# Squares in wide operations, a conditioning visit and the transposes at other places, and the samples' modulation on VectorE, in a decoder step on one core

## The chip, the cores and the metric

The kernel runs on one NeuronCore of a Trainium2 chip. The metric is the device time in microseconds (us) of one execution. In the profile PE is TensorE (PEld its weight loads), DVE is VectorE, ACT is ScalarE, POOL is GpSimd, and SP is the engine that issues most DMAs. All five run their own instruction list strictly in its order and wait for each other through semaphores.

## The reference

One layer for 256 prompt tokens and 8 x 4 sample tokens (288 columns in all), width 2048. Each of the nine sequences (one prompt, eight samples) has its own conditioning row `c`. Cut to what the change touches:

```python
mod = (silu(c) @ w_ada + b_ada)            # per sequence: 6 x 2048
sh_m, sc_m, gt_m, sh_f, sc_f, gt_f = split(mod)
h = rms(x, g_mix) * (1 + sc_m) + sh_m
proj = h @ w_in                            # 2048 x 9216: b, c, hc, u, v, ga, gb
ya = b * short_conv(c * hc)
u, v = gelu(u), rms(gelu(v), g_v)          # v by rows of tokens: its transpose is needed
yb = u * (causal(w_sg) @ v + b_sg)
merged = sigmoid(ga) * (ya @ w_pa) + sigmoid(gb) * (yb @ w_pb)
x = x + gt_m * (merged @ w_out)
h2 = rms(x, g_ffn) * (1 + sc_f) + sh_f
x = x + gt_f * ((silu(gate(h2)) * up(h2)) @ w_ffn_out)
y = rms(x, g_final)
```

## The kernel before

Activations lie transposed, 16 tiles `x[:, k, :]` of 128 features by 288 tokens. Every large product is done in three passes of rounded fp32 parts: `triple` issues three matmuls of 288 columns (lines 214, 215 and 216). The weight's parts come from `Blk.split`: ACT casts 512 columns of a `raw` tile into `hi` (line 393), DVE subtracts to get `lo` (line 395). There are four `hi` and four `lo` buffers, four PSUM banks for products (`pm`), three for small results (`px`), one for the conditioning product (`ada`), and a ring of seven `raw` tiles of 1 MB into which the weights are loaded ahead.

The steps run as a list. TensorE's order is written by hand; the order on the other engines is chosen when the program is built, and is fixed after that. The list begins so:

- `warm` issues matmuls on a constant (line 454) while the first loads are under way.
- `squares1` squares the 16 tiles of x, on DVE (line 461) and ACT (line 463) in turns, and sums each over the features with three one-column matmuls into one PSUM bank (line 465). `roots` makes the reciprocal root from it (DVE line 191, POOL line 194), and `norm1` spreads that over the partitions (line 203) and copies it to `rb` (line 478).
- `Ada` steps multiply conditioning rows by blocks of `w_ada` (line 329). Their `tail` copies the result (`ev`, line 344), turns it on TensorE (line 351), and adds the bias into `mod` (line 355). A run of such steps between two products is called a visit below. `aA` gives shift and scale of tile 0 only, `aB` those of tiles 1 and 2, `aC` those of tiles 3 to 6, `aD` of 7, and `aE` of 8 to 15.
- `mk_h1` makes `gm` (line 486) and calls `modulate`: per tile a product with `rb` (line 247, DVE), the affine step of the 256 prompt columns (lines 257 and 258, ACT), that of the 32 sample columns (lines 261 and 262, POOL), a cast (line 266, ACT) and a subtraction (line 271, DVE). `mk_h2` calls the same for the second half of the layer, 16 tiles, while the four `KBlk` steps of `fk` run.
- The product with `w_in` is cut by input tiles so that it can start before the conditioning is done: six blocks `wA` use tile 0 alone (eight output tiles each, one triple per output tile), then `wB` uses tiles 1 and 2, `wX` 0 to 2, `wC` 3 to 7, `wD` 8 to 15. The first ones write `part` (lines 503 and 505, ACT and DVE), later ones add to it (line 508). `at` says after how many blocks a visit stands.
- In the `wD` stage `sinkD` calls `mix_conv` for 8 output tiles (a dozen DVE operations each, lines 533 to 548). `mix_conv` copies the samples' conv state from the constants `cp` into `zs` (line 537), a copy that needs nothing else. `v_transpose` queues 12 pairs of transposes (line 569), one pair after every second triple, and a DVE operation empties each pair's `px` bank (line 571).

Loads: `load_x`, then the first seven steps' `raw` tiles, with the second pack of constants `cp` behind `wA[0]` (line 797). Each later step's tile is loaded seven steps ahead, as soon as its place in the ring is free.

## Time and profile before

| | |
|---|---|
| runs | 1675.88, 1673.26, 1675.97 us; median 1675.88 |
| profiled execution | 1675.97 us, of which the span of its instructions is 1674.2 us |
| PE busy | 1650.9 us |
| DVE busy | 988.3 us |
| ACT busy | 743.4 us |
| POOL busy | 45.7 us |

A row of the timeline gives the start in us, the duration, the engine, the source line, the operation, output and inputs, and in brackets how long the engine had been idle and what ended that. A PE matmul's shown end is modelled, so busy PE time also holds stretches at a low rate; starts are what to read there. A row of the windows gives for each engine the busy time and the number of instructions in a stretch, and the clock that TensorE was granted. Line numbers of the profile are those of the kernel before.

### The profile page before, as it was taken

The numbers are of one execution on the slowest core, as the hardware profiler recorded it, in microseconds if no ns is written. First come the engines' busy times: TensorE is split into PE (matmuls) and PEld (weight loads), VectorE is DVE, ScalarE is ACT, GpSimd is POOL, SyncE is SP. The second block draws the span as 40 slices with busy tenths as digits, with TensorE's granted clock in tenths as the row PEclk, the third lists the DMA queues.
The fourth block names the chain that finished last, engine by engine and source line by source line (L and its number), as shares of the span: only waits on it lengthen the run. The fifth ranks groups of instructions, "written<-read, shape, count | busy, mean of one in ns | idle before, by whom it ended". The sixth has DMA issues, their size and how long they took to land.

```text
span 1674.2 us, 31388 instructions
## 1 busy us (share of the span) xinstructions
PE 1650.9 (99%) x12584; PEld 1582.2 (95%) x12584; DVE 988.3 (59%) x2011; ACT 743.4 (44%) x1373; POOL 45.7 (3%) x126
## 2 busy tenths in 40 slices
PE   9999999999999999999999999999999999999997
PEld 8899999998989999899989999999999999999997
DVE  3675556877755566667854455555555555555565
ACT  3444334543344434446734444444444444444453
POOL 0000001000000000002300000000000000000000
PEclk9999999999999999999999999999999999999998
DMA  6776776766678666664478546453464534654341
GB/s 267 280 294 236 303 279 244 267 249 234 255 285 325 253 225 251 253 242 163 152 283 308 205 157 218 163 173 116 156 217 169 168 121 156 214 173 159 116 155 57
DMA packets 57266, 357.61 MB, mean 214 GB/s; under 512 B 6400, under 2 KB 9376, under 8 KB 24352
## 3 DMA queue, kind: packets, MB, share of 16 engines
q1 hardware_dynamic: 56832, 355.38, 58.3%
q8 instruction: 98, 1.61, 0.4%
q14 instruction: 48, 0.39, 0.1%
q10 hardware_dynamic: 288, 0.22, 0.0%
HBM read 352.49 MB, written 3.09 MB: 212 GB/s over the span
## 4 chain that ended last, share of the span: by engine, by line
issue 50%; PE 47%; DVE 1%; ACT 1%; POOL 1%; DMA 0%; POOLq 0%; DVEq 0%; ACTq 0%
PE pm L214 14%; PE pm L216 13%; PE pm L215 13%; PE ada L329 4%; PE px L465 1%; DVE x L722 0%; DVE lo L395 0%; PE px L351 0%; PE px L203 0%; POOL t L261 0%; DMA ct<-in_c 0%; ACT hi L393 0%; POOL t L262 0%; PE px L609 0%; PE px L611 0%
## 5 line engine op out<-in xcount | busy, mean ns | idle before, releaser
L214 PE MATMUL pm<-s,hi 128*128 128x288 f32 (+1 forms) x3760 | 1115.1, 297 | 5.3 <-ACT s L503 2.6
L216 PE MATMUL pm<-s,lo 128*128 128x288 f32 (+1 forms) x3760 | 1111.2, 296 | 0.2 <-DVE lo L395 0.2
L215 PE MATMUL pm<-s,hi 128*128 128x288 f32 (+1 forms) x3760 | 1109.5, 295 | 0.0
L393 ACT CAST hi<-raw 128x512 fp32r<-128x512 f32 (+1 forms) x966 | 588.6, 610 | 814.1 <-PE pm L215 778.9
L395 DVE TENSOR_TENSOR lo<-raw,hi 128x512 fp32r<-128x512 f32 (+1 forms) x966 | 655.4, 679 | 492.4 <-ACT hi L393 477.6
L214 PEld LDWEIGHTS pm<-s,hi 128*128 128x128 f32 x3760 | 708.0, 188 | 23.7 <-issue 15.3
L215 PEld LDWEIGHTS pm<-s,hi 128*128 128x128 f32 x3760 | 708.4, 188 | 0.2 <-DVE s L271 0.2
L216 PEld LDWEIGHTS pm<-s,lo 128*128 128x128 f32 x3760 | 707.9, 188 | 0.4 <-DVE lo L395 0.4
L329 PE MATMUL ada<-raw,cs 128*32 128x512 f32 (+2 forms) x960 | 89.6, 519 | 0.0
L508 DVE TENSOR_TENSOR s<-pm,s 128x288 f32<-128x288 f32 x120 | 54.2, 454 | 41.2 <-PE pm L216 41.1
L329 PEld LDWEIGHTS ada<-raw,cs 128*32 128x32 f32 x960 | 29.1, 113 | 43.7 <-issue 38.5
L516 DVE TENSOR_TENSOR s<-pm,s 128x288 f32<-128x288 f32 x72 | 32.8, 456 | 15.9 <-PE pm L216 15.8
L240 ACT CAST s<-t 128x288 fp32r<-128x288 f32 (+1 forms) x76 | 32.6, 432 | 16.1 <-DVE t L548 7.4
L242 DVE TENSOR_TENSOR s<-t,s 128x288 fp32r<-128x288 f32 (+1 forms) x76 | 34.5, 458 | 6.4 <-ACT s L240 6.4
L287 DVE SCALAR_TENSOR_TENSOR x<-pm,mod,x 128x256 f32<-128x256 f32 x80 | 38.0, 475 | 0.0
L694 DVE SCALAR_TENSOR_TENSOR t<-t,pm 128x288 f32<-128x288 f32 x42 | 19.1, 454 | 16.2 <-PE pm L216 16.2
L286 DVE TENSOR_TENSOR t<-pm,mod 128x32 f32<-128x32 f32 x80 | 15.3, 192 | 22.0 <-PE pm L216 22.0
L194 POOL TENSOR_TENSOR r<-e,mhalf 128x3 f32<-128x3 f32 x4 | 3.4, 858 | 899.0 <-DVE e L193 873.5
L153 ACT ACTIVATE t<-x 128x288 f32<-128x288 f32 x30 | 13.4, 445 | 20.8 <-DVE x L288 20.8
L465 PEld LDWEIGHTS px<-ones,t 128*128 128x128 f32 x96 | 20.6, 333 | 1.5 <-ACT t L463 1.5
L465 PE MATMUL px<-ones,t 128*128 128x1 f32 x96 | 20.6, 352 | 1.0 <-ACT t L463 1.0
L158 DVE TENSOR_TENSOR acc<-acc,t 128x288 f32<-128x288 f32 x34 | 15.5, 455 | 8.2 <-ACT t L153 8.2
(108 smaller groups left out, 455.3 us busy)
## 6 DMA issues: line engine op xcount, KB each, us to landing
raw<-in_fi SPq DMA_DIRECT2D x84, 1024.0 KB, 4.9
raw<-in_a SPq DMA_DIRECT2D x64, 1024.0 KB, 9.9
raw<-in_f SPq DMA_DIRECT2D x64, 704.0 KB, 4.0
raw<-in_wD SPq DMA_DIRECT2D x36, 1024.0 KB, 5.0
raw<-in_wC SPq DMA_DIRECT2D x24, 960.0 KB, 4.9
raw<-in_aE SPq DMA_DIRECT2D x16, 1024.0 KB, 8.7
raw<-in_wo SPq DMA_DIRECT2D x16, 1024.0 KB, 5.0
raw<-in_aC SPq DMA_DIRECT2D x8, 1024.0 KB, 8.8
```

Source lines behind the costliest of these rows:

```text
L214: PE.matmul(out, wh, ah, start=first, stop=False)
L215: PE.matmul(out, wh, al, start=False, stop=False)
L216: lh = PE.matmul(out, wl, ah, start=False, stop=last)
L240: A.copy(hi, a)
L242: V.tensor_tensor(lo, a, hi.bitcast(F32), ALU.subtract)
L287: V.scalar_tensor_tensor(x[:, m, :TP], ps[:, :TP], mod[:, gt0 + m, 0:1], x[:, m, :TP], ALU.mult, ALU.add)
L329: PE.matmul(acc[32 * j : 32 * j + 32, :w], cs[:, kt, :], self.raw[:, o : o + w], start=(kt < ks), stop=(kt >= 16 - ks), tile_position=(0, ...
L393: A.copy(hi, self.raw[:, s * 128 : e * 128])
L395: V.tensor_tensor(lo, self.raw[:, s * 128 : e * 128], hi.bitcast(F32), ALU.subtract)
L465: PE.matmul(got["ps"][:, tb : tb + 1], q[:, o : o + 128], ones[:, 0:1], start=k == 0 and tb == 0, stop=k == 15 and tb == 2, skip_group_che ...
L508: V.tensor_tensor(part[m], ps[:, :T], part[m], ALU.add)
L516: V.tensor_tensor(a, ps[:, :T], a, ALU.add)
```

## The change

1. x is loaded in four pieces (5, 5, 4 and 2 tiles) instead of five. ACT squares each piece in one operation, into four tiles of the `raw` ring. DVE adds the first three pieces together, so that three tiles are left of 14; the last piece's two tiles stay as they are. The sums over features need 5 x 3 one-column matmuls instead of 16 x 3. The two late tiles are summed first (`sums1(True)`), the three others (`sums1(False)`) halfway through `aA[0]`, behind three more `warm` matmuls.
2. `aA` has two blocks of 1 MB, each loaded in two halves, instead of four of 512 KB. `norm1` stands halfway through `aA[1]`. The first `warm` has 50 matmuls instead of 14, and two stand ahead of `aA`'s tail.
3. The load of `cp` is issued behind `squares1`, after the first three steps' loads; the next four steps' loads stand behind it and share the ring with the squares.
4. The visit `aB` with `mk_h1(1, 3)` stands after the third block of `wA`, not the fourth.
5. `v_transpose` stands after `wD(40, 44)`, no longer in the loop of the `mix_conv` tiles.
6. The samples' affine step goes from POOL to DVE, in all 32 tiles of `h1` and `h2`.

```diff
@@ -30,7 +30,7 @@
 C_GFFN, C_GFIN, C_WCONV, C_STATE, C_MASK, C_MASKS, C2_END = np.cumsum([0, 16, 16, 24, 128, 128, 32]).tolist()
 
 ADA_UNITS = [
-    ("aA", (16, 16, 0, 0), 1, 4),
+    ("aA", (16, 16, 0, 0), 1, 8),
     ("aB", (17, 17, 1, 1), 2, 4),
     ("aC", (19, 21, 3, 5), 2, 2),
     ("aD", (23, 23, 7, 7), 1, 8),
@@ -44,6 +44,7 @@
 
 TB = (0, 128, 160)
 EARLY = 48
+XCUT = (0, 5, 10, 14, 16)
 
 STREAMS = {
     "wA": (0, 1, 8),
@@ -125,7 +126,7 @@
     x = const("x", [P, 16, T])
 
     def load_x():
-        for a, b in ((0, 3), (3, 7), (7, 11), (11, 14), (14, 16)):
+        for a, b in zip(XCUT, XCUT[1:]):
             SY.dma_start(x[:, a:b, :], d["x"][:, a:b, :])
 
     ones = const("ones", [P, P])
@@ -258,8 +259,8 @@
             A.activation(
                 h[:, :TP], t[:, :TP], AF.Identity, bias=mod[:, sh0 + k, 0:1], scale=gm[:, k, 0:1]
             )
-            G.tensor_tensor(sam(h[:, TP:]), sam(t[:, TP:]), bc4(gm[:, k, 1:]), ALU.mult)
-            G.tensor_tensor(sam(h[:, TP:]), sam(h[:, TP:]), bc4(mod[:, sh0 + k, 1:]), ALU.add)
+            V.tensor_tensor(sam(h[:, TP:]), sam(t[:, TP:]), bc4(gm[:, k, 1:]), ALU.mult)
+            V.tensor_tensor(sam(h[:, TP:]), sam(h[:, TP:]), bc4(mod[:, sh0 + k, 1:]), ALU.add)
             if k == 0 and out is h1:
                 A.copy(hi[:, TP:], h[:, TP:])
             else:
@@ -312,10 +313,14 @@
             self.ks = 2 if self.fb[0] == self.fb[1] else 1
             n = self.nk * 512 * self.nq // self.ks
             self.raw = pw.tile([P, n], F32, tag="raw", name=nm("raw"), bufs=RAW, padded_shape=[P, 2048])
-            SY.dma_start(self.raw, d[self.name][self.blk])
+            w = 1024 if self.name == "aA" else n
+            for o in range(0, n, w):
+                SY.dma_start(self.raw[:, o : o + w], d[self.name][self.blk][:, o : o + w])
 
         def split(self):
             pass
+
+        half = None
 
         def run(self):
             w, ks = self.nq * 128, self.ks
@@ -323,6 +328,8 @@
                 Ada.cur[self.name] = pps.tile([P, 512], F32, tag="ada", name=nm("ada"), bufs=1)
             acc = Ada.cur[self.name]
             for k in range(self.nk // ks):
+                if self.half and 2 * k * ks == self.nk:
+                    self.half()
                 for j in range(4):
                     kt = self.blk * self.nk + k * ks + j % ks
                     o = (k * 4 + j) * w
@@ -455,22 +462,33 @@
 
     def squares1():
         got = S["r1"] = {"ps": psmisc()}
-        for k in range(16):
-            q = tmp()
-            if k % 2:
-                V.tensor_tensor(q, x[:, k, :], x[:, k, :], ALU.mult)
-            else:
-                A.activation(q, x[:, k, :], AF.Square)
+        qs = []
+        for a, b in zip(XCUT, XCUT[1:]):
+            q = pw.tile([P, 2048], F32, tag="raw", name=nm("q"), bufs=RAW)
+            q = q[:, : (b - a) * T].rearrange("p (k t) -> p k t", t=T)
+            A.activation(q, x[:, a:b, :], AF.Square)
+            qs.append(q)
+        q = S["early"] = qs[0]
+        S["late"] = qs[3]
+        V.tensor_tensor(q, q, qs[1], ALU.add)
+        V.tensor_tensor(q[:, 0:4], q[:, 0:4], qs[2], ALU.add)
+        V.tensor_tensor(q[:, 0:2], q[:, 0:2], q[:, 2:4], ALU.add)
+
+    def sums1(late):
+        got = S["r1"]
+        for q in [S["late"][:, i] for i in range(2)] if late else [S["early"][:, i] for i in (0, 1, 4)]:
             for tb, o in enumerate(TB):
                 PE.matmul(
                     got["ps"][:, tb : tb + 1],
                     q[:, o : o + 128],
                     ones[:, 0:1],
-                    start=k == 0 and tb == 0,
-                    stop=k == 15 and tb == 2,
+                    start=not got.get("on"),
+                    stop=False,
                     skip_group_check=True,
                 )
-        roots(got, D, False, False)
+                got["on"] = True
+        if not late:
+            roots(got, D, False, False)
 
     def norm1():
         ps = rstd_bcast(S["r1"])
@@ -735,16 +753,18 @@
         return out
 
     aA, aB, aC, aD, aE = ada("aA"), ada("aB"), ada("aC"), ada("aD"), ada("aE")
-    aA[3].defer = True
+    aA[1].defer = True
+    aA[0].half = lambda: (warm(3), sums1(False))
+    aA[1].half = norm1
     wA = [Blk("wA", i, rh1, sinkA) for i in range(EARLY // 8)]
     wB = [Blk("wB", i, rh1, sinkB) for i in range(EARLY // 8)]
     wX = [Blk("wX", i, rh1, lambda m, ps: sinkA(EARLY + m, ps)) for i in range((72 - EARLY) // 4)]
     wC = [Blk("wC", i, rh1, sinkB) for i in range(24)]
     wA[0].defer, wA[0].cut = True, 512
-    steps = [Do(lambda: warm(14)), Do(squares1), aA[0], Do(norm1)] + aA[1:]
-    steps += [Do(lambda: wA[0].split(1)), Do(lambda: aA[3].tail(0)), Do(lambda: warm(8))]
+    steps = [Do(lambda: warm(50)), Do(lambda: sums1(True))] + aA
+    steps += [Do(lambda: wA[0].split(1)), Do(lambda: warm(2)), Do(lambda: aA[1].tail(0)), Do(lambda: warm(8))]
     steps += [mk_h1(0, 1), Do(lambda: wA[0].split())]
-    steps += at(wA, {4: aB + [mk_h1(1, 3)]})
+    steps += at(wA, {3: aB + [mk_h1(1, 3)]})
     steps += at(wB + wX, {2: aC[:4], 5: aC[4:] + [mk_h1(3, 7)], 8: aD + [mk_h1(7, 8)]})
     steps += at(wC, {3: aE[:4], 8: aE[4:8], 13: aE[8:12], 17: aE[12:] + [mk_h1(8, 12), mk_h1(12, 16)]})
 
@@ -754,9 +774,7 @@
     steps2 = wD(32, 40) + wD(24, 26) + [Do(v_stats)] + wD(26, 32)
     for j in range(0, 8, 2):
         steps2 += wD(j, j + 2) + wD(8 + j, 10 + j) + wD(16 + j, 18 + j)
-        if j == 2:
-            steps2.append(Do(v_transpose))
-    steps2 += wD(40, 72) + [Do(sg_load)]
+    steps2 += wD(40, 44) + [Do(v_transpose)] + wD(44, 72) + [Do(sg_load)]
     sp = {2 + i // 2 + i % 2 * 0: [] for i in range(8)}
     for g in range(8):
         sp[2 + g // 2].append(spatial(g))
@@ -791,10 +809,12 @@
     stream = [s for s in steps if not isinstance(s, Do)]
     pos = {id(s): i for i, s in enumerate(stream)}
     load_x()
-    for s in stream[:AHEAD]:
+    for s in stream[:3]:
         s.load()
-        if s is wA[0]:
-            SY.dma_start(cp, d["cpack2"])
+    squares1()
+    SY.dma_start(cp, d["cpack2"])
+    for s in stream[3:AHEAD]:
+        s.load()
     blks = [s for s in stream if isinstance(s, Blk)]
     nxt, cur = 0, 0
     for s in steps:
```

How this moves the instructions is shown at three places. First the start. On DVE, before, from the last square to the two `zs` copies (`e` is the first step of the root, `s` the normalised tile 0, `cp_74` the first pack of constants, `cp` the second):

```order
L461 TENSOR_TENSOR t_206<-x 128x288
L191 TENSOR_SCALAR e_212<-px_130 128x3
L247 TENSOR_TENSOR s_232<-x,rb_230 128x288
L355 TENSOR_TENSOR mod<-px_270,cp_74 128x9 x2
L486 SCALAR_TENSOR_TENSOR gm_89<-mod,cp_74 128x9
L395 TENSOR_TENSOR lo_266<-raw_108,hi_264 128x512
L537 COPY zs_4552<-cp 128x8x2
L537 COPY zs_4597<-cp 128x8x2
```

The same engine now, from the first sum of squares (`q_109`, `q_111`, `q_113` are the first three pieces' squares) to the root:

```order
L473 TENSOR_TENSOR q_109<-q_109,q_111 128x1440
L555 COPY zs_4536<-cp 128x8x2
L555 COPY zs_4581<-cp 128x8x2
L474 TENSOR_TENSOR q_109<-q_109,q_113 128x1152
L402 TENSOR_TENSOR lo_248<-raw_105,hi_246 128x512
L475 TENSOR_TENSOR q_109<-q_109 128x576
L402 TENSOR_TENSOR lo_278<-raw_105,hi_276 128x512
L192 TENSOR_SCALAR e_209<-px_108 128x3
```

The two copies from `cp` now stand between the first and the second sum, and a `lo` of `wA[0]` stands ahead of the third. TensorE there, before, from the last sum over features to the end of `aA` (`px_226` is the spread of the root `r_211`):

```order
L465 MATMUL px_130<-ones,t_206 128x1 x3
L329 MATMUL ada_217<-raw_100,cs 32x128 x8
L203 MATMUL px_226<-cp_74,r_211 128x128 x2
L203 MATMUL px_226<-cp_74,r_211 128x32
L329 MATMUL ada_217<-raw_102,cs 32x128 x8
L329 MATMUL ada_217<-raw_104,cs 32x128 x8
L329 MATMUL ada_217<-raw_106,cs 32x128 x8
```

TensorE now, from the sums of `q_109`:

```order
L481 MATMUL px_108<-ones,q_109 128x1 x9
L336 MATMUL ada_187<-raw_99,cs 32x128 x8
L336 MATMUL ada_187<-raw_102,cs 32x128 x8
L204 MATMUL px_230<-cp_74,r_208 128x128 x2
L204 MATMUL px_230<-cp_74,r_208 128x32
L336 MATMUL ada_187<-raw_102,cs 32x128 x8
```

Only 9 sums are left behind the DVE chain, one half block of `aA` follows the spread instead of three blocks, and two halves stand between sums and spread.

Second, ACT at the visit `aB`. Before, from the copy of the conditioning product (`ev`) on; `hi_472` to `hi_534` are the casts of the two blocks behind the visit, `t` and `s_610`, `s_616` the modulation of tiles 1 and 2:

```order
L344 COPY ev_577<-ada_538 128x256
L393 CAST hi_472<-raw_354 128x512
L393 CAST hi_476<-raw_354 128x512
L393 CAST hi_530<-raw_412 128x512
L393 CAST hi_534<-raw_412 128x512
L503 COPY s_591<-pm_587 128x288
L258 ACTIVATE t_609<-s_605,mod,gm_89 128x256
L258 ACTIVATE t_615<-s_607,mod,gm_89 128x256
L266 CAST s_610<-t_609 128x288
L266 CAST s_616<-t_615 128x288
L393 CAST hi_657<-raw_470 128x512
L503 COPY s_629<-pm_625 128x288
```

Now, from the cast of the second block behind the visit (`hi_456`) on:

```order
L400 CAST hi_456<-raw_338 128x512
L400 CAST hi_460<-raw_338 128x512
L351 COPY ev_503<-ada_464 128x256
L521 COPY s_517<-pm_513 128x288
L400 CAST hi_583<-raw_396 128x512
L259 ACTIVATE t_535<-s_531,mod,gm_89 128x256
L259 ACTIVATE t_541<-s_533,mod,gm_89 128x256
L267 CAST s_536<-t_535 128x288
L267 CAST s_542<-t_541 128x288
L521 COPY s_555<-pm_551 128x288
L521 COPY s_561<-pm_557 128x288
L521 COPY s_567<-pm_563 128x288
```

The casts of the next two blocks now stand ahead of `ev`, and those of the third (`hi_583`) behind it; three copies out of PSUM (`s_555` and on) still stand behind both modulation casts. DVE there now, from `mod` on, with the samples' steps (lines 262 and 263) among it:

```order
L362 TENSOR_TENSOR mod<-px_525,cp_74 128x18 x2
L504 SCALAR_TENSOR_TENSOR gm_89<-mod,cp_74 128x18
L248 TENSOR_TENSOR s_531<-x,rb_234 128x288
L248 TENSOR_TENSOR s_533<-x,rb_234 128x288
L262 TENSOR_TENSOR t_535<-s_531,gm_89 128x32
L402 TENSOR_TENSOR lo_585<-raw_396,hi_583 128x512
L263 TENSOR_TENSOR t_535<-t_535,mod 128x32
L262 TENSOR_TENSOR t_541<-s_533,gm_89 128x32
L263 TENSOR_TENSOR t_541<-t_541,mod 128x32
L272 TENSOR_TENSOR s_547<-t_535,s_536 128x288
L272 TENSOR_TENSOR s_549<-t_541,s_542 128x288
L523 COPY s_573<-pm_569 128x288
```

What moved: four more DVE operations and the `lo` of a later block stand ahead of the subtractions (line 272).

Third, DVE where the transposes were emptied before, behind the end of a `mix_conv` (`t_4872`):

```order
L548 TENSOR_TENSOR t_4872<-t_4872,s_328 128x288
L516 TENSOR_TENSOR s_334<-pm_4902,s_334 128x288
L537 COPY zs_5140<-cp 128x8x2
L537 COPY zs_5185<-cp 128x8x2
L242 TENSOR_TENSOR s_4882<-t_4872,s_4880 128x288
L571 SCALAR_TENSOR_TENSOR s_4912<-px_4909,r_4113,s_4073 128x256
L571 SCALAR_TENSOR_TENSOR s_4923<-px_4920,r_4113,s_4073 128x256
L571 SCALAR_TENSOR_TENSOR s_4935<-px_4932,r_4113,s_4073 32x256
L571 SCALAR_TENSOR_TENSOR s_4948<-px_4945,r_4113,s_4075 128x256
L571 SCALAR_TENSOR_TENSOR s_4960<-px_4957,r_4113,s_4075 128x256
```

DVE now, where they are emptied (`s_667` to `s_685` are the sums of the gate tiles of `wD(40, 44)`):

```order
L534 TENSOR_TENSOR s_679<-pm_5518,s_679 128x288
L402 TENSOR_TENSOR lo_5489<-raw_5292,hi_5487 128x512
L589 SCALAR_TENSOR_TENSOR s_5598<-px_5595,r_4097,s_4057 128x256
L589 SCALAR_TENSOR_TENSOR s_5609<-px_5606,r_4097,s_4057 128x256
L402 TENSOR_TENSOR lo_5549<-raw_5401,hi_5547 128x512
L589 SCALAR_TENSOR_TENSOR s_5621<-px_5618,r_4097,s_4057 32x256
L534 TENSOR_TENSOR s_685<-pm_5588,s_685 128x288
L589 SCALAR_TENSOR_TENSOR s_5635<-px_5632,r_4097,s_4059 128x256
L402 TENSOR_TENSOR lo_5553<-raw_5401,hi_5551 128x512
L589 SCALAR_TENSOR_TENSOR s_5647<-px_5644,r_4097,s_4059 128x256
L589 SCALAR_TENSOR_TENSOR s_5659<-px_5656,r_4097,s_4059 32x256
L402 TENSOR_TENSOR lo_5557<-raw_5401,hi_5555 128x512
```

The 12 operations that empty the banks now stand apart, with a `lo` or a sum between them, and no operation of `mix_conv` ahead of them.

## Prediction

> **What bounds the kernel now.** I read the page first: busy time and share of each engine, then the waits, the timeline around the longest waits of PE, the windows there, and last the timeline of the start.
>
> ```profile
> span 1674.2 us, 31388 instructions
> PE 1650.9 (99%) x12584; PEld 1582.2 (95%) x12584; DVE 988.3 (59%) x2011; ACT 743.4 (44%) x1373; POOL 45.7 (3%) x126
> ```
>
> PE has work almost throughout and its products are unchanged, so the change can only win what PE loses: in waits, at a low clock, and in the start, whose busy time is not product work. After the first product the timeline has four waits of PE that are longer than 0.5 us and lie before the last normalisation:
>
> ```profile
> 53.62 0.41 PE L214 MATMUL pm<-s,hi 128*128 128x288 f32 x1 [1.01 <-ACT hi L393]
> 60.14 0.40 PE L214 MATMUL pm<-s,hi 128*128 128x288 f32 x1 [2.56 <-ACT s L503]
> 113.32 0.37 PE L214 MATMUL pm<-s,hi 128*128 128x288 f32 x1 [1.71 <-DVE s L508]
> 412.04 0.41 PE L569 MATMUL px<-cp,s 128*128 128x128 f32 x2 [3.99 <-DVE s L571]
> ```
>
> The first two stand behind the visit `aB`, the third behind `aC`, the fourth in the transposes. The windows show what follows a wait:
>
> ```profile
> core 0: us, PE busy (x) PEld busy (x) DVE busy (x) ACT busy (x) POOL busy (x), PEclk, DMA share, GB/s
> 57.90:61.30 3.40, 1.16 (x8) 1.17 (x9) 1.95 (x5) 3.38 (x10) 0.74 (x4) 1.00 1.02 426
> 61.30:64.70 3.40, 3.40 (x17) 3.40 (x16) 2.14 (x4) 2.10 (x7) 0.00 (x0) 0.50 1.01 424
> 109.10:112.50 3.40, 2.51 (x20) 2.28 (x18) 3.17 (x8) 2.92 (x8) 1.77 (x4) 1.00 1.02 426
> 409.50:412.90 3.40, 0.86 (x7) 0.89 (x8) 3.33 (x11) 0.43 (x1) 0.00 (x0) 1.00 0.05 19
> 412.90:416.30 3.40, 3.40 (x17) 3.37 (x16) 1.40 (x4) 0.62 (x1) 0.00 (x0) 0.50 0.29 92
> 809.10:832.40 23.30, 23.30 (x172) 23.30 (x171) 21.01 (x46) 21.06 (x49) 13.71 (x32) 1.00 0.40 136
> ```
>
> Behind the waits of 2.56 and 3.99 us the clock is 0.50 for 3.4 us, which loses 1.7 us each. In the 3.4 us before, PE was busy for 1.16 and 0.86 us. Where it was busy for 2.51 us (109.1), the clock stayed at 1.00. So the transposes cost 3.99 + 1.7 and the visit `aB` 1.01 + 2.56 + 1.7. The last row gives the pace used below: 172 matmuls in 23.3 us, about 0.4 us for a triple.
>
> **The start.** The first product starts at 34.73 us:
>
> ```profile
> 5.66 20.64 PE L465 MATMUL px<-ones,t 128*128 128x1 f32 x96 [0.99 <-ACT t L463]
> 26.23 1.08 PE L329 MATMUL ada<-raw,cs 128*32 128x128 f32 x16
> 27.49 1.78 PE L203 MATMUL px<-cp,r 128*128 128x128 f32 x6 [0.18 <-POOL r L194]
> 29.20 2.79 PE L329 MATMUL ada<-raw,cs 128*32 128x128 f32 x48
> 32.06 0.27 ACT L344 COPY ev<-ada 128x128 f32<-128x128 f32 x1 [2.35 <-PE ada L329]
> 34.73 0.61 PE L214 MATMUL pm<-s,hi 128*128 128x288 f32 x1
> 802.46 0.56 PE px L178 x6
> ```
>
> The 48 sums take 20.64 us, 0.43 us each. Now there are 15, and 9 of them wait for the three DVE additions. When do these end? DVE's list has two `zs` copies between the first and the second addition, and they need `cp`:
>
> ```profile
> 9.24 0.33 SPq L797 DMA_DIRECT2D cp<-in_cpack  x1
> cp<-in_cpack SPq DMA_DIRECT2D x1, 172.0 KB, 7.6
> 33.92 0.29 DVE L537 COPY zs<-cp 128x16 f32<-128x16 f32 x2
> 4.95 0.32 ACT L138 ACTIVATE ctt<-ct 128x144 f32<-128x144 f32 x1 [2.01 <-DMA ct<-in_c]
> L463 ACT ACTIVATE t<-x 128x288 f32<-128x288 f32 x8 | 3.4, 439 | 10.5 <-PE px L465 9.8 <-DMA x<-in_x 0.7
> L461 DVE TENSOR_TENSOR t<-x 128x288 f32<-128x288 f32 x8 | 3.7, 458 | 14.6 <-PE px L465 10.7 <-DMA x<-in_x 3.9
> L395 DVE TENSOR_TENSOR lo<-raw,hi 128x512 fp32r<-128x512 f32 x878 | 606.3, 692 | 444.0 <-ACT hi L393 429.3
> x<-in_x SPq DMA_DIRECT2D x1, 288.0 KB, 7.2
> ```
>
> `cp` landed at 9.24 + 7.6 = 16.8 us, behind x, `aA` and `wA[0]`. Now the same bytes are ahead of it, so 16.8 again. The squares are ready long before: the last of x lands 7.2 us after an issue near 2.8, at 10; ACT's rows of 144 and 288 elements (0.32 and 0.44) give 0.83 ns an element, so the four squares of 1440, 1440, 1152 and 576 take 1.4, 1.4, 1.2 and 0.7 us and end by about 11.5. DVE's rows of 288 and 512 (0.458, 0.692) give 1.04 ns an element: 1.65, 1.36 and 0.76 us for the additions. Behind the first one DVE stands until 16.8; then copies to 17.15, second addition to 18.45, `lo` (0.69) to 19.1, third addition to 19.8.
>
> PE, idle since about 14, then makes 9 sums at 0.43: 23.7. At the rate of the row of 802.46 (six records are three sums, 0.19 each) they would take 1.7 us instead of 3.9; PE will have stood idle for some 6 us, so I take 0.43. Two halves of `aA` follow, 32 records at 2.79/48 = 0.058: 25.5. The root takes 27.49 - 26.30 = 1.2 us behind the sums, 24.9, so it is hidden. The spread starts at 25.5, the last half of `aA` 1.7 later (29.20 - 27.49), and ends at 28.15. From there to the first product it was 34.73 - 31.99 = 2.74 us; the chain of copy, turn, `mod`, `gm` and ACT's affine step is the same, the two `warm` add under 0.1, and POOL's samples step was not what ACT's cast waited for. First product at 31.0: **3.8 us saved**. Bounds: 2.2 more if the sums run fast; some 2 more if the copies hold nothing up (then the `lo` of `wA[0]`, loaded just ahead of `cp`, still comes first); the other way, each us that `cp` lands later costs one. The first products run slowly until the clock comes up, now as before; by where that falls, one stretch of 3.4 us at half clock, 1.7 us, may be gained or lost.
>
> **The visit aB.** The casts of the next two blocks now stand ahead of `ev`, so the wait of 1.01 goes. What of the 2.56? Counted from the visit's end:
>
> ```profile
> 55.38 0.51 PE L351 MATMUL px<-cp,ev 128*128 128x18 f32 x4
> 56.74 0.25 DVE L355 TENSOR_TENSOR mod<-px,cp 128x18 f32<-128x18 f32 x2
> 56.94 0.18 DVE L486 SCALAR_TENSOR_TENSOR gm<-mod,cp 128x18 f32<-128x18 f32 x1
> 57.04 0.82 DVE L247 TENSOR_TENSOR s<-x,rb 128x288 f32<-128x288 f32 x2
> 58.52 0.75 ACT L266 CAST s<-t 128x288 fp32r<-128x288 f32 x2
> ```
>
> Three triples (1.2) and the turn (0.51) bring 1.7, `mod` and `gm` 2.1, the two products with `rb` 2.9. On DVE then a sample step, the `lo` of a later block (0.69; it waits for ACT until 2.7), and three more sample steps: 4.0. A sample step is priced by DVE's own row on 128x32 below, 0.18 busy. ACT casts both tiles to 4.6 and only then copies `s_555` out of PSUM, to 4.95. PE has banks for three more triples, to 3.2, and waits for that copy until 5.0: 1.8 us left. So **2.0 us saved** in waits. The clock is open: 1.8 idle of 3.4 lies between the rows above; I take half, **0.85 saved**.
>
> The Trainium skill, "TensorE: Matmul & The Clock Gate", section "Why this matters for your kernels", says only idle gaps above about 3 us drop the clock. This trace has a drop behind 2.56 us, so the limit is lower here. By the page this visit would save the whole 1.7, 0.85 more than I sum.
>
> **The visit aC.** Same walk: PSUM copies stood behind subtractions that waited for POOL. Now they stand behind eight sample steps, two `rb` products and two `lo`: the copy that frees the fourth bank (`s_679`) starts at 6.85 after the visit, PE wants it at 5.9 and gets it at 7.3, 1.4 instead of 1.71. **0.3 saved**; between 1.7 saved and 1 lost.
>
> **The transposes.** Before, the emptying stood behind a whole `mix_conv` on DVE:
>
> ```profile
> 411.41 1.91 DVE L571 SCALAR_TENSOR_TENSOR s<-px,r,s 128x256 f32<-128x256 f32 x4
> ```
>
> Now PE gives a pair every two triples, about 1.05 us; DVE must do one emptying (0.48) and on average half a `lo` (0.35) and a tenth of a us of sums: 0.94. It keeps up, with three banks of slack, and the visit `a3` just before, in which PE needs neither `lo` nor banks, lets it catch up. The wait and its slow clock go, and what took DVE's time there, `mix_conv`, runs as in the other three pairs, where PE did not wait. **5.7 us saved.** If it does not keep up, up to 4 of it come back.
>
> **The samples on DVE.**
>
> ```profile
> L262 POOL TENSOR_TENSOR t<-t,mod 128x32 f32<-128x32 f32 x32 | 13.9, 437 | 2.2
> L395 DVE TENSOR_TENSOR lo<-raw,hi 128x512 fp32r<-128x512 f32 x13 | 9.1, 709 | 1.4 <-ACT hi L393 1.2
> L703 DVE TENSOR_TENSOR s<-s,w 128x32 f32<-128x32 f32 x4 | 0.7, 184 | 0.0
> 828.54 0.29 PE L214 MATMUL pm<-s,hi 128*128 128x288 f32 x1
> 831.26 0.46 DVE L271 TENSOR_TENSOR s<-t,s 128x288 fp32r<-128x288 f32 x1 [0.18 <-ACT s L266]
> ```
>
> 16 tiles of `h2` add 32 operations from 809 to 832, where DVE is busy 21.0 of 23.3 us. Back to back they cost about 0.12 each, 3.8 us, of which the 2.3 idle take part. The last tile was done at 831.7; the product that starts at 828.54 reads it as its 16th, at 834.5. Of 2.8 us cover 1.5 to 3.8 are used: between nothing and 1 lost. In `wC` seven tiles add 14 more, 1.7 us, where an output tile has five triples (2 us) and three banks wait behind it, up to 6 us of cover. **0.5 lost** in all; bounds 0 and 3.
>
> The Trainium skill, "SBUF — State Buffer", section "Who interferes with whom", says that a DVE operation with two SBUF inputs and a POOL operation that reads SBUF exclude each other. The `lo` of that stretch bear it out a little: 0.709 on average (the row of 13) against 0.692 in all. By the page DVE's 46 operations there would each get that back, 46 x 0.02 = 0.9 us, an estimate, and this term would be 0.
>
> **Sum.** 3.8 + 2.0 + 0.85 + 0.3 + 5.7 - 0.5 = 12.15. The profiled execution took 1675.97 (span 1674.2 and 1.8 around it), by the median of the runs, 1675.88: 1675.97 - 12.15 = **1663.8**.
>
> **Rivals.**
> - All waits go: my walks are too strict, the remaining 1.8 + 0.85 of `aB` and 1.4 of `aC` vanish, and the sums start at 17.8 or run fast: 1663.8 - 6 = 1657.8. For it: a walk adds up small overlaps, and tenths decide. Against: the order is fixed and the copies out of PSUM do stand behind. 0.15.
> - New waits: the emptying of transposes meets late `lo` on DVE (4 back) and `aB` keeps its slow clock (0.85): 1668.7. 0.15.
> - DVE becomes the bound in 809 to 832. Each step there waits for the one before and for ACT's cast; if a step costs what POOL's did (0.44), 32 cost 14 us, less 2.3 and 2.8: 9 lost there, and in `wC` 6 less 2: about 1676, no change. From 0.5 us a step on the result is slower by over 0.2%; at 0.75, 19 and 8 are lost, 1691. Against: 0.184 measured on DVE. 0.03 for slower, 0.04 for about the same.
> - The change does not do what it says, since `cp` lands later than 16.8 and holds all sums: each us is lost one for one, but at most to the old 34.7: 1667.6. 0.05.
>
> **How the numbers follow.** The forecast of 1663.8 within 2.5 has 0.58; within it the clock behind `aB` drops (1664.6) or holds (1662.9) at even odds, and the page's rule named there is the second of these. Forecast and the nearer parts of the first two rivals give 1658.5 to 1670 with 0.85. About 0.2% (3.35 us) is what a measurement can tell here; faster by that needs under 1672.5: 0.92; within 0.2%: 0.05; slower: 0.03.
>
> **What would show it.** Right: the `zs` copies start at about 16.9 and the second addition behind them; first product near 31; no wait over 0.5 us at the transposes and no window at 0.50 there; behind `aB` one wait near 1.8 that an ACT copy ends; no wait at 834. Wrong: a first product above 33 or below 28.5, a wait above 1 us at a transposes' bank, or a PE wait for a subtraction of line 272 in `h2`.

## The result, and the profile after

The changed kernel takes 1658.36 us (median of four runs, 1657.81 to 1658.83), the kernel before 1675.9 beside it: ratio 0.9899, interval 0.9882 to 0.9916. The forecast was 1663.8 with a range from 1658.5; the median lies 5.4 us below the forecast and 0.1 us below that range. The two profiled executions, 1675.97 and 1658.83, differ by 17.1 us where 12.15 were forecast. The kernel before varies by itself: in the later series its 9, 7 and 21 runs have medians of 1675.71, 1673.49 and 1673.45 and reach from 1670.29 to 1676.19, so beside the last two of them the gain is nearer 15 us.

The page of the changed kernel, to be set beside the two lines of before:

```profile
span 1657.1 us, 31287 instructions
PE 1633.0 (99%) x12559; PEld 1563.6 (94%) x12559; DVE 992.7 (60%) x2070; ACT 745.1 (45%) x1369; POOL 20.0 (1%) x62
```

PE's busy time fell by 17.9 us. Of that, 10.6 us lie ahead of the first product (32.05 before, 21.43 now), where there are fewer sums and more idle time; 7.2 us lie behind it, where the products are the same (as before, busy time contains what is lost at a low clock). Its timeline in the start:

```profile
12.96 0.54 PE L461 MATMUL pm<-wb 128*128 128x288 bf16 x3
20.10 4.00 PE L481 MATMUL px<-ones,q 128*128 128x1 f32 x18 [6.60 <-DVE q L475]
24.03 1.93 PE L336 MATMUL ada<-raw,cs 128*32 128x128 f32 x32
25.89 1.78 PE L204 MATMUL px<-cp,r 128*128 128x128 f32 x6
31.39 0.40 PE L215 MATMUL pm<-s,hi 128*128 128x288 f32 x1
```

And DVE's, ahead of the sums:

```profile
9.07 1.66 DVE L473 TENSOR_TENSOR q<-q,q 128x1440 f32<-128x1440 f32 x1 [2.88 <-ACT q L469]
17.27 0.25 DVE L555 COPY zs<-cp 128x16 f32<-128x16 f32 x2 [6.54 <-DMA cp<-in_cpack]
17.43 1.35 DVE L474 TENSOR_TENSOR q<-q,q 128x1152 f32<-128x1152 f32 x1
18.69 0.69 DVE L402 TENSOR_TENSOR lo<-raw,hi 128x512 fp32r<-128x512 f32 x1
19.30 0.75 DVE L475 TENSOR_TENSOR q<-q 128x576 f32<-128x576 f32 x1
```

The first sum is done early; then DVE stands for 6.54 us at a copy that needs `cp` and that nothing near it needs. The nine sums behind the third addition take 4.00 us, 0.44 each; the granted clock is 0.50 from 14.05 to 31.12, with these sums in it. The first product starts at 31.39 instead of 34.73.

Only two waits of PE over 0.5 us are left between the first product and the last normalisation:

```profile
50.08 0.40 PE L215 MATMUL pm<-s,hi 128*128 128x288 f32 x1 [1.50 <-ACT s L521]
103.67 0.40 PE L215 MATMUL pm<-s,hi 128*128 128x288 f32 x1 [1.26 <-DVE s L526]
```

The windows, with PE's granted clock behind the busy times:

```profile
core 0: us, PE busy (x) PEld busy (x) DVE busy (x) ACT busy (x) POOL busy (x), PEclk, DMA share, GB/s
27.70:31.10 3.40, 3.40 (x27) 2.11 (x28) 1.21 (x6) 1.63 (x4) 0.00 (x0) 0.50 1.00 422
31.10:34.50 3.40, 3.31 (x23) 2.81 (x21) 1.67 (x4) 1.58 (x6) 0.00 (x0) 1.00 1.00 416
48.20:51.60 3.40, 1.90 (x14) 1.66 (x14) 2.58 (x9) 3.31 (x10) 0.00 (x0) 1.00 1.01 426
458.30:461.70 3.40, 3.40 (x29) 3.40 (x28) 2.92 (x7) 1.41 (x3) 0.00 (x0) 1.00 1.01 422
792.40:815.60 23.20, 23.20 (x170) 23.04 (x169) 21.63 (x72) 20.18 (x45) 0.00 (x0) 1.00 0.40 137
```

The clock is up when the first product starts, it does not fall behind the visit `aB`, and in the transposes (458) and in the stage of `h2` (792) PE has no idle time.

The last triple starts 17.2 us earlier. Where they went is found by counting: PE's 3776 triples come in the same order in both kernels, so the distance of two triples can be compared directly. For the rest of the run behind the transposes, the 961st and the last triple are, before and after:

```profile
484.26 0.29 PE L214 MATMUL pm<-s,hi 128*128 128x288 f32 x1
1659.32 0.30 PE L214 MATMUL pm<-s,hi 128*128 128x288 f32 x1
```

```profile
469.46 0.29 PE L215 MATMUL pm<-s,hi 128*128 128x288 f32 x1
1642.12 0.30 PE L215 MATMUL pm<-s,hi 128*128 128x288 f32 x1
```

1175.06 us have become 1172.66, although PE is shown idle for 0.0 us of this stretch in either kernel: the same products follow each other a little closer. This is called the pace below. The table gives all stretches:

| stretch | forecast, us saved | between the two profiles |
|---|---|---|
| up to the first product | 3.8 | 3.34 |
| its first three triples (clock) | 0, by up to 1.7 either way | 0.92 |
| visit `aB` | 2.85 | 4.01 |
| visit `aC` | 0.3 | 0.50 |
| triples 151 to 801 | 0 | 0.33 |
| triples 801 to 961, the transposes | 5.7 | 5.70 |
| triples 961 to the last | -0.5 (samples, with `wC`) | 2.39 |

### The profile page after: what moved, and what is told of

Read it like the earlier page. It is cut to its first block, busy times and chain, and to the rows that moved or that the text cites. A ratio compares the mean times of both kernels' runs of the same rounds, so it can differ in the third digit from the quotient of the medians.

```text
span 1657.1 us, 31287 instructions
## 1 busy us (share of the span) xinstructions
PE 1633.0 (99%) x12559; PEld 1563.6 (94%) x12559; DVE 992.7 (60%) x2070; ACT 745.1 (45%) x1369; POOL 20.0 (1%) x62
## 4 chain that ended last, share of the span: by engine, by line
issue 52%; PE 46%; DMA 1%; DVE 1%; ACT 1%; POOLq 0%; POOL 0%; ACTq 0%; DVEq 0%; SPq 0%
PE pm L215 14%; PE pm L216 13%; PE pm L217 13%; PE ada L336 4%; DMA raw<-in_wA 1%; DMA cp<-in_cpack 0%; DVE x L740 0%; PE px L358 0%; PE px L481 0%; PE px L204 0%; DVE lo L402 0%; ACT hi L400 0%; PE px L627 0%; PE px L629 0%; PE px L587 0%
## 5 line engine op out<-in xcount | busy, mean ns | idle before, releaser
L521 ACT COPY s<-pm 128x288 f32<-128x288 f32 x45 | 17.0, 399 | 6.7 <-PE pm L217 6.7
L523 DVE COPY s<-pm 128x288 f32<-128x288 f32 x27 | 12.3, 456 | 11.5 <-PE pm L217 11.5
L259 ACT ACTIVATE t<-s,mod,gm 128x256 f32<-128x256 f32 x32 | 18.2, 596 | 2.1 <-DVE s L248 2.1
```

## The experiments: parts undone and parts alone

The changed kernel takes 1658.36; it was measured in its own series only, so differences from it of some tenths of a us are not to be trusted without a trace. The first four kernels ran together, beside nine runs of the kernel before with a median of 1675.71.

**e1, the transposes at the old place:**

```diff
         steps2 += wD(j, j + 2) + wD(8 + j, 10 + j) + wD(16 + j, 18 + j)
+        if j == 2:
+            steps2.append(Do(v_transpose))
-    steps2 += wD(40, 44) + [Do(v_transpose)] + wD(44, 72) + [Do(sg_load)]
+    steps2 += wD(40, 72) + [Do(sg_load)]
```

> The changed kernel with the transposes back between the mix_conv tiles. If the wait of 3.99 us at an emptied bank and the 3.4 us at clock 0.50 behind it belong to that place, both return: 5.4 to 5.7 us above the changed kernel, about 1664.0, and a window at 0.50 near 395 us. Rival: the place costs nothing by itself now that other work has moved; no wait and about 1658.4. The even gain of 2.4 us that the two profiles show between the transposes and the end (the same matmuls 0.2% apart in pace) should stay if it belongs to the run or to another edit.

Measured 1663.02 (1661.91 to 1665.27; ratio to before 0.9934, interval 0.9920 to 0.9948). Its timeline of PE at the transposes:

```profile
401.86 0.41 PE L587 MATMUL px<-cp,s 128*128 128x128 f32 x2 [3.98 <-DVE s L589]
```

The wait is back, and the clock is 0.50 from 402.5 to 405.9; the triples 801 to 961 take 80.23 us against 74.51, 5.72 more. The median is 4.7 higher; the profiled execution, the fastest of the five at 1661.91, is only 3.1 above the changed kernel's 1658.83, because other stretches are shorter in it: the first product starts at 30.31 (1.08 earlier), the last stretch takes 1171.83 instead of 1172.66, and what follows the last triple takes 0.74 less.

**e2, the visit behind the fourth block again:**

```diff
-    steps += at(wA, {3: aB + [mk_h1(1, 3)]})
+    steps += at(wA, {4: aB + [mk_h1(1, 3)]})
```

> The changed kernel with the visit aB back behind the fourth block of wA. If the visit's place makes the waits of 1.01 and 2.56 us and the slow stretch of 1.7 us, against one wait of 1.50 us now, 3.8 us are lost: about 1662.2, with a window at 0.50 near 60 us. Rival: the waits came from POOL's sample steps, which ACT's casts waited for; they are on DVE now, so only the 1.01 returns and no slow window: 1659.4.

Measured 1658.49 (1658.37 to 1658.74): no difference. Neither theory held; PE waits once, for 1.50 us at 53.18, and the clock stays at 1.00. What the visit's place was credited with does not come from it.

**e3, the samples' steps on POOL again:**

```diff
-            V.tensor_tensor(sam(h[:, TP:]), sam(t[:, TP:]), bc4(gm[:, k, 1:]), ALU.mult)
-            V.tensor_tensor(sam(h[:, TP:]), sam(h[:, TP:]), bc4(mod[:, sh0 + k, 1:]), ALU.add)
+            G.tensor_tensor(sam(h[:, TP:]), sam(t[:, TP:]), bc4(gm[:, k, 1:]), ALU.mult)
+            G.tensor_tensor(sam(h[:, TP:]), sam(h[:, TP:]), bc4(mod[:, sh0 + k, 1:]), ALU.add)
```

> The changed kernel with the samples' two steps per tile back on POOL. By the term of the forecast DVE's steps cost 0.5 us in all, so 1657.9, with bounds of 0 and 3 faster. Rival: POOL's work beside DVE slows the subtractions and PE's supply, or the even gain of 2.4 us between 470 us and the end comes from POOL being idle: 1660 to 1661, with the matmuls' pitch as in the kernel before.

Measured 1658.88 (1658.03 to 1659.09): 0.5 slower by the medians, within the spread of the two; the profiled executions, 1658.80 and 1658.83, are the same. By the traces DVE in place of POOL wins 0.4 us from the 4th to the 151st triple, most of it at `aC`, and 0.4 from there to the 801st, and loses 0.6 behind the 961st. The wait at `aC` is 1.70 in its trace, 1.26 in the changed kernel. DVE's groups in the stage of `h2` (792.4 to 815.6), first with POOL at work, then in the changed kernel (the last numbers are busy us and mean ns, then the idle time before them):

```profile
L402 DVE TENSOR_TENSOR lo<-raw,hi 128x512 fp32r<-128x512 f32 x13 | 9.0, 708 | 2.8 <-ACT hi L400 2.6
L248 DVE TENSOR_TENSOR s<-x,rb 128x288 f32<-128x288 f32 x16 | 7.4, 480 | 0.0
L272 DVE TENSOR_TENSOR s<-t,s 128x288 fp32r<-128x288 f32 x13 | 6.0, 468 | 1.6 <-ACT s L267 1.6
```

```profile
L402 DVE TENSOR_TENSOR lo<-raw,hi 128x512 fp32r<-128x512 f32 x14 | 9.6, 687 | 2.6 <-ACT hi L400 2.3 <-issue 0.2
L248 DVE TENSOR_TENSOR s<-x,rb 128x288 f32<-128x288 f32 x15 | 6.5, 452 | 0.0
L272 DVE TENSOR_TENSOR s<-t,s 128x288 fp32r<-128x288 f32 x13 | 5.8, 452 | 0.3 <-ACT s L267 0.3
L262 DVE TENSOR_TENSOR t<-s,gm 128x32 f32<-128x32 f32 x15 | 2.5, 187 | 0.0
L263 DVE TENSOR_TENSOR t<-t,mod 128x32 f32<-128x32 f32 x15 | 2.5, 187 | 0.1
```

With POOL idle DVE's operations on two SBUF tiles are 3 to 6% shorter, and its idle time before the subtractions falls from 1.6 to 0.3 us. So DVE's busy time rises by 1.4 us only, from 20.19 to 21.63 of 23.2 us, although the 30 new operations stand with 5.0 in the rows; PE is busy throughout in both. That is what the Trainium skill, "SBUF — State Buffer", section "Who interferes with whom", would have: a DVE operation with two inputs in SBUF and a POOL operation that reads SBUF get in each other's way. The size here is a few per cent.

**e4, the start alone:** the kernel before with edits 1, 2 and 3, that is e1, e2 and e3 undone together in the changed kernel.

> The kernel before with the new start alone (edits 1, 2 and 3; visit, transposes and samples as before). The first product 3.3 us earlier and at full clock at once (0.9 more): 4.3 us under the kernel before, about 1671.6, with the waits at 56, 109 and 408 us as before. Rival: the even gain of 2.4 us comes with the start as well: 1669.

Measured 1666.84 (1665.97 to 1666.96; ratio 0.9952, interval 0.9940 to 0.9965), 4.8 below the expectation. First product at 30.39, 1.0 us earlier than in the changed kernel. Most of what was not expected is won at the visit `aB`, which stands at its old place here: from the 4th to the 151st triple 74.42 us instead of 78.47. ACT's timeline there in e4, then in the kernel before:

```profile
44.09 2.18 ACT L400 CAST hi<-raw 128x512 fp32r<-128x512 f32 x4
47.41 0.37 ACT L351 COPY ev<-ada 128x256 f32<-128x256 f32 x1 [1.15 <-PE ada L336]
```

```profile
52.68 0.37 ACT L344 COPY ev<-ada 128x256 f32<-128x256 f32 x1 [3.22 <-PE ada L329]
52.95 2.18 ACT L393 CAST hi<-raw 128x512 fp32r<-128x512 f32 x4
```

In e4 the four casts stand ahead of `ev`; before, ACT stood idle for 3.22 us in front of `ev` with the casts behind it. PE's one wait at the visit in e4 is 1.58 us, and the clock stays at 1.00 behind it.

The next three put one edit each into the kernel before; they ran beside 21 runs of it with a median of 1673.45.

**v, the visit alone** (`at(wA, {4:` becomes `at(wA, {3:`):

> The kernel before with edit 4 alone: visit aB behind the third block. Built so, the casts of the next blocks already stand ahead of ev. If that order is what ends the waits of 1.01 and 2.56 us, one wait near 1.8 stays and no window at 0.50 behind it: 3.4 us under the kernel before, 1672.3 against 1675.7; then visit and start each bring the same gain, which counts once. Rival: the waits came from loads that were late in the old start; they stay, 1675.7. If the even 0.2% of pace between 150 us and the end comes with this edit, 2.5 us more.

Measured 1673.13 (1670.91 to 1675.82; ratio 0.9999, interval 0.9990 to 1.0008): nothing. The expectation was wrong on the order, as the timeline of ACT and PE shows:

```profile
47.64 0.37 ACT L344 COPY ev<-ada 128x256 f32<-128x256 f32 x1 [3.22 <-PE ada L329]
47.91 2.18 ACT L393 CAST hi<-raw 128x512 fp32r<-128x512 f32 x4
```

```profile
48.58 0.41 PE L214 MATMUL pm<-s,hi 128*128 128x288 f32 x1 [1.01 <-ACT hi L393]
54.91 0.42 PE L214 MATMUL pm<-s,hi 128*128 128x288 f32 x1 [2.38 <-ACT s L503]
```

`ev` still stands ahead of the casts, with the same idle time, and both waits are there, as is a clock of 0.50 from 55.2 to 58.6. They are not from late loads either: in this trace the loads of the two blocks behind the visit land at 39.98 and 41.22, over 6 us before the casts start. So ACT's order makes these waits, and the new order comes with the start's edits (e4 has it, at the visit's old place; e2 too has one wait of 1.50 us there). Which of the three brings it was not tried apart.

**s, the samples alone** (e3's diff, the other way, in the kernel before):

> The kernel before with edit 6 alone: the samples' two steps on DVE. ACT's order at aB is the old one, ev ahead of the casts, so 1.01 and 2.56 stay; aC's wait falls by 0.4, as between e3 and the changed kernel: 1675.3 against 1675.7. Rival: POOL's steps made the 2.56 us: 1671.5. If the even 0.2% of pace comes with this edit, 2.5 us more.

Measured 1670.29 (1667.59 to 1673.04; ratio 0.9985, interval 0.9975 to 0.9995). The waits at `aB` are as before, 1.01 and 2.59 us; the wait at `aC` falls to 1.26 from 1.71; the rest of what is won is the pace (3.2 us behind the 961st triple).

**t, the transposes alone** (e1's diff, the other way, in the kernel before):

> The kernel before with edit 5 alone: the transposes behind wD(40, 44). The wait of 3.99 and the slow stretch go: 5.5 us under the kernel before, 1670.2 against 1675.7. If the 4.8 us between single runs of the kernel before (1671.3 to 1676.1) come from the drop of the clock there, this kernel's runs lie within 2 us. If the even 0.2% of pace comes with the old place, 2.5 us more: 1667.7.

Measured 1666.78 (1663.18 to 1666.85; ratio 0.9960, interval 0.9947 to 0.9974). The triples 801 to 961 take 74.47, as in the changed kernel, and 3.0 us more are won behind them. Its five runs reach over 3.7 us, not within the 2 expected, so the drop of the clock at the transposes alone does not make the spread of the kernel before.

All fourteen traces, sorted by two edits, settle which edits the pace comes with. The time from the 961st triple to the last is

| samples on | transposes | kernels | us |
|---|---|---|---|
| POOL | old place | before, v, e4 | 1175.06 to 1175.12 |
| DVE | old place | s, e1 | 1171.83 to 1171.85 |
| POOL | new place | t, e3 | 1172.05 to 1172.06 |
| DVE | new place | changed kernel, e2, and e5, e6, e7, e9, e10 below | 1172.65 to 1172.67 |

and from the 151st to the 801st 288.27 to 288.31 with POOL, 287.90 to 287.95 with DVE. Within a group kernels agree to 0.06 us, whatever their start and visit. So the pace is no matter of the run: either edit alone takes about 3 us off, and the two together 2.4. Behind the 961st triple all these kernels have the same triples, with PE shown idle for 0.0 us, and behind the 2400th DVE's and ACT's operations start at the same distance from them, to 0.03 us at the three places compared (kernel before, s and changed kernel). The difference sits in single triples: between the kernel before and s, 321 of 2815 are shorter by 8 to 21 ns, 3.4 us together, many of them in patterns that repeat every 8 or 16 triples. What makes it stays open; where the buffers lie in memory is a guess that no run tested.

## The experiments: the start

These ran beside seven runs of the kernel before with a median of 1673.49 (the last one, e10, with the group above).

**e5, `cp` behind x:**

```diff
     load_x()
+    SY.dma_start(cp, d["cpack2"])
     for s in stream[:3]:
         s.load()
     squares1()
-    SY.dma_start(cp, d["cpack2"])
```

> The changed kernel with the load of cp issued right behind x. If the zs copies that wait for cp hold the additions up, the second addition now ends near 12.2 us; the lo of wA[0] that stands ahead of the third still waits for its cast, to 17.4, so the third ends at 18.2 and the sums start there, 1.8 us earlier. If TensorE's clock still comes up only at 31.1, the first products lose half of what they gain: 1.0 to 1.8 us faster, 1656.6 to 1657.4. Rival: aA or wA, each 0.4 us later, set the start: no gain.

Measured 1656.96 (1656.65 to 1657.15). Its timeline of DVE:

```profile
12.06 1.36 DVE L474 TENSOR_TENSOR q<-q,q 128x1152 f32<-128x1152 f32 x1
17.05 0.69 DVE L402 TENSOR_TENSOR lo<-raw,hi 128x512 fp32r<-128x512 f32 x1 [3.62 <-ACT hi L400]
```

The second addition starts at 12.06 instead of 17.43, the sums at 18.46, the first product at 29.75, and from there on the distance to the changed kernel stays: 1.64 at the first triple, 1.69 at the last. The copy from `cp` did hold the start up, and the `lo` of `wA[0]` holds it up next.

**e6, warm matmuls in the idle time:** `warm(3)` becomes `warm(44)` ahead of `sums1(False)`.

> The changed kernel with 44 instead of 3 warm matmuls ahead of the last sums: they fill TensorE's idle time from 13.5 to 20.1 us (44 at 0.152 are 6.7 us) and change nothing else. If the 0.43 us of a sum and the slow aA halves come from the clock of 0.50 that follows the idle time, the clock stays at 1.00: 9 sums at 0.24 instead of 0.43 give 1.8, 48 matmuls of aA at 0.04 instead of 0.058 to 0.068 give 1.1, the spread and the tail about 1: 4 us faster, 1654.4. Rival: a sum costs 0.43 whatever the clock: within 0.5 us of 1658.4, or later by what the warm matmuls run over.

Measured 1658.3 (1657.65 to 1660.47): nothing won. In its trace `cp` came 0.9 us later, and PE had another pause:

```profile
12.95 6.84 PE L461 MATMUL pm<-wb 128*128 128x288 bf16 x44
21.03 2.77 PE L481 MATMUL px<-ones,q 128*128 128x1 f32 x18 [1.24 <-DVE q L475]
```

The granted clock is 1.00 from 15.59 to 22.41 and 0.50 from there to 32.65. The sums that fell half into each took 2.77 us instead of 4.00, but all steps behind them were slow again. The trial did not do what it was to do, so e7 decides.

**e7, both:** e5's diff, and `warm(3)` becomes `warm(32)`.

> The changed kernel with cp behind x and 32 warm matmuls up to the sums, which now start near 18.2. If the two add: 1.8 and 4, and nothing lost to the clock any more: 5.8 us faster, 1652.6. Rival: the loads become the bound, aB's above all: 1654.4 or less gain.

Measured **1654.0** (1653.86 to 1654.26; ratio to before 0.9885, interval 0.9868 to 0.9901), the fastest of all, 4.4 below the changed kernel. PE's timeline, then a window:

```profile
13.86 6.05 PE L461 MATMUL pm<-wb 128*128 128x288 bf16 x32
19.75 2.06 PE L481 MATMUL px<-ones,q 128*128 128x1 f32 x18
21.74 1.08 PE L336 MATMUL ada<-raw,cs 128*32 128x128 f32 x32
27.10 0.40 PE L215 MATMUL pm<-s,hi 128*128 128x288 f32 x1 [0.71 <-ACT s L265]
```

```profile
17.90:21.30 3.40, 3.40 (x31) 3.04 (x29) 2.31 (x4) 1.14 (x2) 0.00 (x0) 1.00 1.03 408
```

Here the clock holds from 17.9 on. The same nine sums take 2.06 us (4.00 at clock 0.50), 32 matmuls of `aA` 1.08 (1.93), and from the sums' end to the first product it is 5.4 us (7.4). So the 0.44 us of a sum is the clock's doing, as the forecast had it. The sums start 1.3 later than in e5, since the 32 warm ones ran over; even so the median is 3.0 below e5's.

**e9, five tiles:** e5's diff, and

```diff
-        V.tensor_tensor(q[:, 0:2], q[:, 0:2], q[:, 2:4], ALU.add)
-        for q in [S["late"][:, i] for i in range(2)] if late else [S["early"][:, i] for i in (0, 1, 4)]:
+        for q in [S["late"][:, i] for i in range(2)] if late else [S["early"][:, i] for i in range(5)]:
```

> The changed kernel with cp behind x and without the third addition, so that 15 instead of 9 sums stand behind it, but no operation of DVE ahead of them waits for cp or wA[0]. The second addition ends near 12.2 us and PE goes on at once: 15 sums at 0.24 to 0.43 are done at 17.2 to 20.1 instead of 24.0. First product 4 to 7 us earlier: 1651.5 to 1654.5. Rival: the product then waits for wA or the visit for aB, and only part of it, 2 us, is seen: 1656.5.

Measured 1655.23 (1653.85 to 1655.63; ratio 0.9890, interval 0.9876 to 0.9905). The sums start at 13.45, and though six more of them run at the slow clock, 5.94 us in all, the first product starts at 26.67, 4.7 earlier than in the changed kernel, as expected. The median lies 0.7 above the expected range all the same; the trace is that of the fastest of the four.

**e10, warm ones between the sums:** e9 with `warm(60)`, `warm(6)`, and

```diff
                 got["on"] = True
+            if not late:
+                warm(2)
```

> e9 with 60 instead of 50 warm matmuls first, 6 instead of 3 ahead of the 15 sums, and 2 behind each 3 sums, so that TensorE's clock has no reason to fall between 10 us and the first product. If the sums go at 0.22 as in e7 (3.3 us, and 1.3 for the warm ones) and the steps behind them take e7's 5.4 us: first product at 23.5 instead of 26.67, and nothing lost to the clock behind it: 3.5 us under e9, 1651 to 1652. Rival: the sums hold the array so little that the clock falls all the same: 1 us slower than e9 for the added matmuls; or aB's loads, which end near 31, hold the visit up: 1653.5.

Measured 1655.04 (1654.79 to 1655.24): no better than e9. The clock held and the sums were done by 17.4, 2.0 earlier; but the first step of the root stands on DVE behind a `lo` of `wA[0]`, whose cast waits for its load. DVE, ACT and PE:

```profile
20.08 0.69 DVE L402 TENSOR_TENSOR lo<-raw,hi 128x512 fp32r<-128x512 f32 x1 [0.58 <-ACT hi L400]
20.69 0.15 DVE L192 TENSOR_SCALAR e<-px 128x3 f32<-128x3 f32 x1
```

```profile
19.43 1.14 ACT L400 CAST hi<-raw 128x512 fp32r<-128x512 f32 x2 [0.66 <-DMA raw<-in_wA]
```

```profile
22.21 1.35 PE L204 MATMUL px<-cp,r 128*128 128x128 f32 x6 [3.42 <-POOL r L195]
```

The wait moved by one link: PE now stands for 3.42 us at the spread, and the clock falls at 22.7. The rival named in the expectation (sums that hold the array too little) was not the reason, nor were late loads at `aB`, where PE waits for the same 1.50 us.

## Why the prediction was right, and where it was wrong

- **Start: right.** The copies from `cp` were put at 16.8 and came at 17.27, the sums at 19.8 and 20.10, their end at 23.7 and 24.03, the first product at 31.0 and 31.39. e5 shows that the copies are the reason. The closeness has some luck: in the traces of e1 and e4, with the same start, the clock came up at 27.0 and the first product at 30.3 and 30.4.
- **The clock behind the first product: left open, and gained.** The clock came up 0.3 us before the first product instead of 2.7 us behind it (37.4 and 34.73 before). Some of that is luck: in e2 and e3, with the same start, it came up 0.75 and 0.98 us behind the first product, and the first three triples took 1.76 and 1.88 us instead of 1.65 (2.58 before).
- **`aB`: the mechanism right, one size off, the cause credited to the wrong edit.** One wait of 1.50 us remained where 1.8 were forecast, ended by the ACT copy that was named. (The 2.0 counted as saved is not what the forecast's own figures give: 1.01 + 2.56 - 1.8 = 1.77. With 1.50 it is 2.07, so the slip happened to fit.) Half of a 1.7 us clock drop was counted, and none came. The reordering on ACT was read from the whole change, under the visit's name; v and e2 show that the visit's place does nothing and e4 that the start's edits bring the order. The Trainium skill, "TensorE: Matmul & The Clock Gate", section "Why this matters for your kernels", has the clock fall only behind gaps above about 3 us, and 1.50 us without a drop agrees. The drops behind 2.56 and, in v, 2.38 us do not, nor does e6's, behind 1.24 us of idle time and sums of one column.
- **`aC`: right within 0.2.** 0.50 instead of 0.3; e3 shows that moving the samples off POOL is what shortened the wait, from 1.70 to 1.26.
- **Transposes: right.** 5.70 counted, 5.7 forecast; e1 and t have it return and go by the same amount.
- **Samples: wrong, and a step that failed.** The term was -0.5, from 46 added operations on a DVE with 2.3 us to spare in the stage of `h2`. DVE's other operations became shorter with POOL idle, its busy time there rose by 1.4 us only, and PE did not wait (e3). With the new place of the transposes the edit is worth nothing clear of the spread; alone (s) it wins 3.2 us by the medians, most of it as pace.
- **The pace: not in the sum, and the largest step that failed.** "its products are unchanged, so the change can only win what PE loses: in waits, at a low clock, and in the start" left out 2.7 us (0.33 + 2.39) by which the unchanged products themselves run faster. That, with the two gains at the clock (0.92 and 0.85) and 0.5 for the samples, is 5.0 of the 5.05 us between 12.15 and 17.2; smaller misses (0.46 too much in the start, 0.3 and 0.2 too little at the visits) cancel.
- **The rivals.** 1657.8, "all waits go", is nearest in number but did not happen: the waits of 1.50 and 1.26 are there.

## What to carry to other kernels

An engine that works strictly in order is held up by whatever stands ahead: read the whole list between two steps of a chain, not the chain, and expect the next entry to hold it up once the first is gone (the copy from `cp`, then a `lo`, then the root). When several edits land together, what each is worth cannot be read from their joint order: here the new place of a visit was worth nothing, and the start's edits brought the order that ended its waits. A pause on TensorE costs its own length and the slow stretch behind it, so filling it with idle products can pay more than shortening it, if nothing else is left to wait for.

## What the runs showed of the hardware

- The same matmuls in the same order, without idle time of PE, take 1171.83 to 1175.12 us, by which engine does the samples' step and where the transposes stand; within each of the four groups kernels repeat within 0.06 us. The cause is open.
- The granted clock changes on a grid of 3.41 us (its stretches last 3.41, 6.83, 10.24, 13.65 us and so on), whose place differs from run to run: it came up at 27.04 in e1, 31.12 in the changed kernel and 31.97 in e2, which have the same start.
- Behind the first product the clock fell where PE was busy for at most 1.17 us of the 3.41 us ahead (1.16 and 0.84 in the kernel before, 1.03 in v, 0.82 and 1.17 in s, 0.64 in e1), and held with 1.91 (e5, at `aB`). A single wait of 1.50 us leaves that much wherever the grid stands. In the start it also fell behind 2.55 us (changed kernel, at 14.05) and 2.17 us (e6, at 22.41), of which 1.50 and 1.38 us were one-column sums; that such sums count for little fits, and was not tested apart.
- Kernels with pauses that lower the clock spread over 3 to 6 us in their runs (before, v, s, t, e1), though e4, which has one too, stays within 1.0; the changed kernel, e2, e3, e5, e7 and e10, which have none between the first product and the last normalisation, within 1.1 (e9 1.8, e6 2.8). That the grid's place makes this spread fits but was not shown.
